# Transformer trunk on one core: first loads of the down matmul by units, the last gate unit's values in another buffer, and VectorE in place of GpSimd for four products' splits

## The chip, the core and the metric

The kernel runs on one NeuronCore of a Trainium2 chip. Five engines run side by side, each through its own list of instructions in strict order: TensorE (PE in the profile; its weight loads are PEld), VectorE (DVE), ScalarE (ACT), GpSimd (POOL), and SyncE (SP), whose list here holds nearly all transfers between HBM and the on-chip memory SBUF. They wait for one another by semaphores. The metric is the device time of one execution in microseconds; the median of several runs is compared.

## What is computed

A two-layer trunk over 1024 tokens of width 1024. Layer 0 mixes tokens by latent attention, layer 1 by differential attention; each mixer is followed by a layer norm, a SwiGLU feed-forward block with 2816 hidden values, and another layer norm. The change lies in the feed-forward block, which runs once per layer:

```python
def _swiglu(x, w_gu, w_down):
    gate, up = jnp.split(x @ w_gu, 2, axis=-1)
    return (jax.nn.silu(gate) * up) @ w_down

h = _layernorm(ALPHA * h + mix, ln_mix_g[i], ln_mix_b[i])
h = _layernorm(ALPHA * h + _swiglu(h, ffn_w_gu[i], ffn_w_down[i]), ln_ffn_g[i], ln_ffn_b[i])
```

Inputs and output are float32.

## The kernel before

**Splitting.** Each float32 operand of a matmul is split in two parts of the type float32r: ScalarE casts the value (the high part), another engine subtracts the cast from the value (the low part), and three matmuls (high by high, high by low, low by high) replace one. `split` (line 472) does this, and `op_unit` (479) does it into a fresh buffer of 128 x 2 x 512. The list `tags` says from which ring the buffer comes, by turns: "wh" and "wl" are rings of three buffers each in the pool `wp`, which lives through the whole kernel; "o" is a ring of six in a pool of the down matmul.

**Gate and up.** `ffn` (491) works a matrix product with seven products of blocks in place of eight. Its 22 units n (line 510 on) each have the products "1", "6", "2", "7", "5", "4", "3", of 12 matmuls each, taken from `stream` in an order of their own, with the weights of each split four steps ahead (`prepare`, 541, into "wh" and "wl"). The last product, "3", reads b22; "5" reads t1, "7" t3, "4" t4, and "1" and "2" read x (its first and its second half). `tmp[n]` (615) holds the unit's running values: 8 KB in each partition, from a ring of two ("ra" of `pool_a`). When a unit is through, `activations` (620) forms the hidden values of its half: L622 the silu on ScalarE, L626 and L627 two products on VectorE. After each second unit GpSimd forms four sums (L631 to L634, tile `sh`), and hidden values and sums go to HBM (`h_dr`, lines 636 and 637) in the blocks s = 0 to 6 that the down matmul asks for.

**Down.** Seven products again, each of 11 units j, and each unit of 12 matmuls: four blocks of 128 tokens by three. `from_h` (730) loads the hidden values of block s in groups of four, four and three units into a ring of two raw tiles (`rh`) and splits them, VectorE subtracting. The weights come from `b11` (751), `t1`, `t2`, `t3`, `block` ("b21", "b22") and `t4`. `b11` loads the eleven tiles `tt[j]`, 512 KB each, and splits the first half of each; `t1` subtracts one half of `tt[j]` from the other on VectorE (L758) and splits the difference; `t2` works on with `tt` (L764), and `t3` splits what it leaves. GpSimd subtracts for all of these except the first `early` = 3 units of `b11`. The names that the profile has for the seven products, in their order, are dx, dy, dx, dw, dv, dw, dw; all weights of the first, third and fifth appear as op_w_b, those of the others as op_w_t (in layer 1 the last has wt). `whole` (795) runs a product; `added` (804) adds a result to the rows z on VectorE, and `finish` does the layer norm.

**Memory.** A pool that is opened when others have been closed lies over their tiles. The raw tiles `rh` lie over one half of x, `tt0` to `tt3` over the other, `tt4` to `tt7` over the two buffers of `tmp`, `tt8` to `tt10` over t4; z, the "o" ring and the rows g and b lie over t2, t1, b22 and t3. A pool marked `reuse_waits="tile"` has its instructions wait for the old tiles under their own tile.

**Order.** The Tile framework plans each engine's list ahead of time: at each step the engine takes, among the instructions that its plan holds to be ready, the one that stands first in the program or has a higher priority (`tc.high_priority`). `behind` (155) adds that one instruction stands behind another in its list, without a wait. `load_down` (723) uses it to keep the loads of the down matmul in program order, as soon as `in_order` has been filled (834), which is after the first product. The first three units' loads and splits have a high priority. The rows g and b of the layer norm are broadcast into SBUF by two transfers on GpSimd's queue (832, 833).

Of the kernel before, what the change touches and what calls it, by code (L numbers as in the profile page):

```python
# [9 lines left out]
F32 = mybir.dt.float32  # L10
F32R = mybir.dt.float32r
AF = mybir.ActivationFunctionType
ALU = mybir.AluOpType
# [3 lines left out]
P = 128  # L17
S = 1024
D = 1024
# [23 lines left out]
def trunk(  # L43
# [63 lines left out]
    def f32(t):  # L107
        return t.bitcast(F32)
# [363 lines left out]
    def split(dst, src, eng):  # L472
        hi, lo = dst
        A.copy(hi, src)  # L474
        eng.tensor_tensor(lo, src, f32(hi), ALU.subtract)  # L475
# [15 lines left out]
    def ffn(side, xo, xst, pending, layer, x_src, x_dst, lng, lnb, next_x, spare=()):  # L491
# [212 lines left out]
        for i in (1, 0):  # L704
# [5 lines left out]
        poolx = stx.enter_context(tc.tile_pool(name=f"fx{layer}", bufs=1, side=swap(side), reuse_waits="tile"))  # L710
# [10 lines left out]
        chain, in_order, banks_read = [], [], []  # L721

        def load_down(dst, src):

            i = nc.sync.dma_start(dst, src).ins
# [25 lines left out]
        def b11():  # L751
            for j in range(11):
                load_down(tt[j], w_dn[layer, j].rearrange("p (b c) -> p b c", b=2))
                yield unit(tt[j][:, 0], f"b11_{j}", V if j < early else G)

        def t1():
            for j in range(11):
                V.tensor_tensor(tt[j][:, 0], tt[j][:, 1], tt[j][:, 0], ALU.subtract)  # L758
                yield unit(tt[j][:, 0], f"t1_{j}")
# [11 lines left out]
        def block(kh, cs, name):  # L771
            for j, r in enumerate(w_block(kh, cs, name)):
                yield unit(r, f"{name}_{j}")

        def t4():
            for j, r in enumerate(w_block(1, lo_half, "t4")):
# [6 lines left out]
                t = poolx.tile([P, 2, 512], F32R, tag=f"tt{j}", name=f"wt4{layer}_{j}")  # L783
# [69 lines left out]

        y4 = accumulators("w", "y")
# [638 lines left out]
```

## Time and profile before

| | us |
|---|---|
| median of 3 runs | 2299.32 |
| lowest and highest | 2297.55, 2300.04 |
| the profiled execution | 2302.24 |
| its span, first to last instruction | 2300.2 |
| mean granted TensorE clock | 0.993 |

The profile is of one execution. A timeline row has start, length, engine, line, operation, tiles written and read, shape and count, and in brackets the idle time of the engine before it with what ended that. Rows that follow each other are merged (x132), and a merged row lasts from the first start to the last end. Rows "SPq" are the issue of a transfer on SyncE's queue, not its duration. A group of instructions shows busy time and mean duration, or smallest, median and largest. Matmuls overlap: one is shown with 389 ns, and the next starts 227 ns after it where nothing holds it up, so pace is read from start to start.

The four engines' lists meet at the seam between the last gate unit and the first product of the down matmul, at about 873 us in layer 0 and 2071 us in layer 1.

### The profile page before, as it was taken

What the parts mean: (1) busy time and instruction counts of PE and PEld (TensorE: products, weight loads), DVE (VectorE), ACT (ScalarE), POOL (GpSimd) and SP (SyncE); (2) the same over time, 40 slices, a digit from 0 to 9 for tenths busy, and PEclk for the clock granted to TensorE, in tenths of its full rate; (3) what the DMA queues carried; (4) which work ended last, traced back from release to release, by engine and by line L of the source; (5) the groups of instructions that cost most, each with busy time, mean ns of one, the idle gap of its engine ahead of it and who ended that gap; (6) DMA issues with size and microseconds to landing.
All of it is one profiled execution on the core that took longest, in us unless ns stands there. A gap on an engine that the chain in (4) does not pass through costs nothing. (4 is left out here: it accounts for less than half of the span.)

```text
span 2300.2 us, 31168 instructions
## 1 busy us (share of the span) xinstructions
PE 2253.4 (98%) x11410; PEld 1919.6 (83%) x11410; DVE 1551.7 (67%) x2891; ACT 1017.8 (44%) x2096; POOL 863.9 (38%) x688
## 2 busy tenths in 40 slices
PE   8999999999999999999999999999999999999997
PEld 8899997878888887888888898987778888887886
DVE  5667664596666668667476667576586666658777
ACT  4455573342333324445365656555442333324453
POOL 2223241014444445555432424221014444435564
PEclk9999999999999999999999999999999999999999
DMA  5010125434435338544310212053344232337453
GB/s 200 14 36 30 41 72 180 138 128 142 178 133 197 128 111 327 198 171 156 94 54 19 70 38 69 16 214 139 108 160 149 76 120 87 125 127 284 160 205 121
DMA packets 105545, 288.28 MB, mean 125 GB/s; under 512 B 7968, under 2 KB 30112, under 8 KB 94896
## 3 DMA queue, kind: packets, MB, share of 16 engines
q1 hardware_dynamic: 100976, 275.87, 33.5%
q0 software_dynamic: 4416, 10.42, 1.7%
q8 instruction: 90, 1.47, 0.3%
q14 instruction: 63, 0.52, 0.1%
HBM read 205.00 MB, written 77.07 MB: 123 GB/s over the span
## 5 line engine op out<-in xcount | busy, mean ns | idle before, releaser
L474 ACT CAST op_g<-gr 128x512 fp32r<-128x512 f32 x240 | 147.0, 621 | 376.5 <-PE gb L520 188.4
L475 POOL TENSOR_TENSOR op_g<-gr,op_g 128x512 fp32r<-128x512 f32 x104 | 144.0, 1390 | 254.2 <-ACT op_g L474 140.7
L475 DVE TENSOR_TENSOR op_h<-rh,op_h 128x512 fp32r<-128x512 f32 x154 | 157.8, 1055 | 68.2 <-ACT op_h L474 68.2
L520 PE MATMUL ga<-xh_m,op_g 128*128 128x512 f32 x512 | 168.1, 389 | 0.0
L474 ACT CAST op_h<-rh 128x512 fp32r<-128x512 f32 x154 | 92.7, 619 | 147.5 <-PE dx L790 41.1
L790 PE MATMUL dw<-op_w_t,op_h 128*128 128x512 f32 x660 | 151.1, 390 | 0.0
L790 PEld LDWEIGHTS dw<-op_w_t,op_h 128*128 128x128 f32 x660 | 123.6, 188 | 25.6
L222 ACT ACTIVATE l_b<-l_b,mx_b 128x256 f32<-128x256 f32 (+7 forms) x128 | 99.5, 778 | 78.9 <-DVE mx_b L219 77.1
L1297 POOL TENSOR_SCALAR l_b<-l_b,r_b,cst 128x128 f32<-128x128 f32 (+3 forms) x64 | 52.8, 824 | 204.1 <-DVE r_b L224 193.5
L790 PE MATMUL dx<-op_w_b,op_h 128*128 128x512 f32 x528 | 124.4, 397 | 5.0 <-ACT op_w_b L474 3.9
L475 POOL TENSOR_TENSOR op_w_t<-tt,op_w_t 128x512 fp32r<-128x512 f32 x66 | 98.6, 1497 | 80.5 <-ACT op_w_t L474 79.9
L790 PEld LDWEIGHTS dx<-op_w_b,op_h 128*128 128x128 f32 x528 | 101.1, 192 | 28.0 <-ACT op_w_b L474 4.7
L475 DVE TENSOR_TENSOR op_g<-gr,op_g 128x512 fp32r<-128x512 f32 x136 | 111.4, 821 | 17.6 <-ACT op_g L474 17.4
L520 PE MATMUL gc<-b22h_f,op_g 128*128 128x512 f32 x352 | 115.6, 389 | 2.5 <-ACT op_g L474 2.5
L520 PE MATMUL gb<-t3h_f,op_g 128*128 128x512 f32 x352 | 115.6, 390 | 2.2 <-ACT tmp L622 1.6
L520 PE MATMUL gb<-t4h_f,op_g 128*128 128x512 f32 x352 | 115.8, 390 | 1.3 <-DVE tmp L603 1.3
L475 POOL TENSOR_TENSOR op_g<-s,op_g 128x512 fp32r<-128x512 f32 x40 | 54.6, 1365 | 166.0 <-ACT op_g L474 158.0
L520 PE MATMUL gc<-t1h_f,op_g 128*128 128x512 f32 x352 | 115.9, 390 | 0.6 <-ACT op_g L474 0.5
L520 PE MATMUL gb<-t2h_f,op_g 128*128 128x512 f32 x352 | 115.2, 390 | 0.4 <-DVE op_g L475 0.4
L520 PEld LDWEIGHTS ga<-xh_m,op_g 128*128 128x128 f32 x512 | 96.1, 188 | 20.0
L143 PE MATMUL bp<-xT_f,h_wb 128*128 128x512 f32 x256 | 103.7, 405 | 0.0
L145 PE MATMUL bp<-xT_f,l_wb 128*128 128x512 f32 x256 | 102.0, 399 | 0.0
(376 smaller groups left out, 6749.6 us busy)
## 6 DMA issues: line engine op xcount, KB each, us to landing
gr<-in_w_gu SPq DMA_DIRECT2D x44, 1024.0 KB, 6.9
rh<-h_dr SPq DMA_DIRECT2D x28, 1024.0 KB, 5.1
h_dr<-sh SPq DMA_DIRECT2D x22, 1024.0 KB, 5.0
h_dr<-hp SPq DMA_DIRECT2D x22, 768.0 KB, 4.1
tt<-in_w_dn SPq DMA_DIRECT2D x22, 512.0 KB, 7.9
rh<-h_dr SPq DMA_DIRECT2D x14, 768.0 KB, 4.3
wo_dr<-op_pwo SPq DMA_DIRECT2D x16, 512.0 KB, 3.4
z<-xs_dr SPq DMA_DIRECT2D x16, 512.0 KB, 10.1
```

Of the source, the lines that this page charges most:

```text
L143: T.matmul(ps_out, lh, rh, start=(i == 0), stop=False)
L145: T.matmul(ps_out, ll, rh, start=False, stop=(i == n - 1))
L222: A.activation(l[:, :n], l[:, :n], AF.Exp, bias=mx, scale=-1.0, accum_out=sm)
L474: A.copy(hi, src)
L475: eng.tensor_tensor(lo, src, f32(hi), ALU.subtract)
L520: T.matmul(o, w[:, a, kc], x[b][:, k, :], start=(first and k == 0 and (a, b) == (0, 0)), stop=(k == 3 and a == 1), skip_group_check=True,)
L790: T.matmul(o, h[:, a, c], w[:, b_], start=(first and (a, b_) == (0, 0)), stop=(last and a == 1), skip_group_check=True,)
L1297: G.tensor_scalar(l1[:, :n], l1[:, :n], r1, nlam, ALU.mult, ALU.mult)
```

## The change

- `from_h` can load unit by unit (`one`), 256 KB each in place of 1 MB, and the first product does so; its first `early` = 2 units, and those of `b11`, are split into the ring ("wh", "wl") alone. They are traced by turns, one of the hidden values and one of the weights, at a high priority.
- `tmp` of the last unit (n = 21) comes from the ring of five big tiles (`big_tile`, 8 KB each, which also holds the gate weights `gr`, `hp`, `sh` and later the raw weights `rw`).
- The eleven `tt` tiles come from two pools, one of eight and one of three, at the same places as before.
- `load_down` keeps program order from the first load on.
- VectorE subtracts for all splits of b11, t1, b21 and b22 (and `b11` also subtracts one half of `tt[j]` from the other, which `t1` did). GpSimd keeps t2, t3 and t4.
- The broadcasts of g and b are traced behind the third product, inside `tc.issue_after(turns["last"])`, which puts what is traced in the block on the engine of the given instruction behind that instruction; `turns["last"]` is the subtraction of the latest `op_unit`.

```diff
     def split(dst, src, eng):
         hi, lo = dst
         A.copy(hi, src)
-        eng.tensor_tensor(lo, src, f32(hi), ALU.subtract)
+        return eng.tensor_tensor(lo, src, f32(hi), ALU.subtract).ins
...
-        split((t[:, 0], t[:, 1]), src, eng)
+        i = split((t[:, 0], t[:, 1]), src, eng)
+        turns["last"] = i
         return t
...
         def new_tmp(n):
-            tmp[n] = pool_a.tile([P, 4, 512], F32, tag="ra", name=f"tmp{layer}_{n}", bufs=2)
+            if n == NFF - 1:
+                tmp[n] = big_tile(f"tmp{layer}_{n}", F32).rearrange("p a (b c) -> p (a b) c", b=2)
+            else:
+                tmp[n] = pool_a.tile([P, 4, 512], F32, tag="ra", name=f"tmp{layer}_{n}", bufs=2)
...
-        poolx = stx.enter_context(tc.tile_pool(name=f"fx{layer}", bufs=1, side=swap(side), reuse_waits="tile"))
+        poolx = [
+            stx.enter_context(tc.tile_pool(name=f"f{n}{layer}", bufs=1, side=swap(side), reuse_waits="tile"))
+            for n in "ex"
+        ]
+        js = [range(8), range(8, 11)]
+        if swap(side) != "left":
+            js = [reversed(r) for r in js]
...
         tt = {
-            j: poolx.tile([P, 2, 512], F32, tag=f"tt{j}", name=f"tt{layer}_{j}")
-            for j in (range(11) if swap(side) == "left" else reversed(range(11)))
+            j: p.tile([P, 2, 512], F32, tag=f"tt{j}", name=f"tt{layer}_{j}") for p, r in zip(poolx, js) for j in r
         }
...
             i = nc.sync.dma_start(dst, src).ins
-            if in_order:
+            if chain:
                 behind(i, chain[-1])
             chain.append(i)
...
-        def from_h(s, name, tags=tags):
+        def from_h(s, name, tags=tags, one=False):
             for gi, (j0, j1) in enumerate(groups):
                 r = poolh.tile([P, 4, 512], F32, tag="rawh", name=f"rh{layer}_{name}_{gi}")
-                load_down(r[:, :j1 - j0], h_dr[gi][s, :, :j1 - j0, :])
+                if not one:
+                    load_down(r[:, :j1 - j0], h_dr[gi][s, :, :j1 - j0, :])
                 for j in range(j0, j1):
-                    yield op_unit(r[:, j - j0], V, f"h{layer}_{name}_{j}", tags, pool)
+                    if one:
+                        load_down(r[:, j - j0], h_dr[gi][s, :, j - j0, :])
+                    yield op_unit(r[:, j - j0], V, f"h{layer}_{name}_{j}", ring if one and j < early else tags, pool)
...
         def b11():
             for j in range(11):
                 load_down(tt[j], w_dn[layer, j].rearrange("p (b c) -> p b c", b=2))
-                yield unit(tt[j][:, 0], f"b11_{j}", V if j < early else G)
+                w = unit(tt[j][:, 0], f"b11_{j}", V, ring if j < early else tags)
+                V.tensor_tensor(tt[j][:, 0], tt[j][:, 1], tt[j][:, 0], ALU.subtract)
+                yield w
 
         def t1():
             for j in range(11):
-                V.tensor_tensor(tt[j][:, 0], tt[j][:, 1], tt[j][:, 0], ALU.subtract)
-                yield unit(tt[j][:, 0], f"t1_{j}")
+                yield unit(tt[j][:, 0], f"t1_{j}", V)
...
         def block(kh, cs, name):
             for j, r in enumerate(w_block(kh, cs, name)):
-                yield unit(r, f"{name}_{j}")
+                yield unit(r, f"{name}_{j}", V)
...
-        early = 3
+        early, ring = 2, ("wh", "wl")
...
-        hs, ws = from_h(0, "1"), b11()
+        hs, ws = from_h(0, "1", one=True), b11()
         with tc.high_priority(100):
-            hs, ws = (itertools.chain([next(x) for _ in range(early)], x) for x in (hs, ws))
+            first = [(next(hs), next(ws)) for _ in range(early)]
+        hs, ws = (itertools.chain([u[i] for u in first], x) for i, x in enumerate((hs, ws)))
...
-        g = bcast_row(pool, lng, D, f"fg{layer}", "g")
-        b = bcast_row(pool, lnb, D, f"fb{layer}", "b")
-        in_order.append(True)
...
+        with tc.issue_after(turns["last"]):
+            g = bcast_row(pool, lng, D, f"fg{layer}", "g")
+            b = bcast_row(pool, lnb, D, f"fb{layer}", "b")
         y4 = accumulators("w", "y")
         whole(y4, from_h(4, "6"), t2(), True)
```

More of the change, by code (lines that the diff above doesn't have):

```diff
@@ L716, in ffn @@
         tt = {
-            j: poolx.tile([P, 2, 512], F32, tag=f"tt{j}", name=f"tt{layer}_{j}")
-            for j in (range(11) if swap(side) == "left" else reversed(range(11)))
+            j: p.tile([P, 2, 512], F32, tag=f"tt{j}", name=f"tt{layer}_{j}") for p, r in zip(poolx, js) for j in r
         }
-        chain, in_order, banks_read = [], [], []
+        chain, banks_read = [], []
         def load_down(dst, src):
             i = nc.sync.dma_start(dst, src).ins
-            if in_order:
+            if chain:
                 behind(i, chain[-1])
             chain.append(i)
-        def from_h(s, name, tags=tags):
+        def from_h(s, name, tags=tags, one=False):
             for gi, (j0, j1) in enumerate(groups):
                 r = poolh.tile([P, 4, 512], F32, tag="rawh", name=f"rh{layer}_{name}_{gi}")
-                load_down(r[:, :j1 - j0], h_dr[gi][s, :, :j1 - j0, :])
+                if not one:
+                    load_down(r[:, :j1 - j0], h_dr[gi][s, :, :j1 - j0, :])
                 for j in range(j0, j1):
-                    yield op_unit(r[:, j - j0], V, f"h{layer}_{name}_{j}", tags, pool)
+                    if one:
+                        load_down(r[:, j - j0], h_dr[gi][s, :, j - j0, :])
+                    yield op_unit(r[:, j - j0], V, f"h{layer}_{name}_{j}", ring if one and j < early else tags, pool)
         def w_block(kh, cs, name):
@@ L782, in t4 @@
                     continue
-                t = poolx.tile([P, 2, 512], F32R, tag=f"tt{j}", name=f"wt4{layer}_{j}")
+                t = poolx[j > 7].tile([P, 2, 512], F32R, tag=f"tt{j}", name=f"wt4{layer}_{j}")
                 split((t[:, 0], t[:, 1]), r, G)
```

## The prediction

> **What bounds the kernel now.** I read the page first, for the engine that sets the time, then the list of who waited for whom on TensorE, then TensorE's timeline at the places that the list names, and last the queues that feed those places.
>
> ```profile
> PE 2253.4 (98%) x11410; PEld 1919.6 (83%) x11410; DVE 1551.7 (67%) x2891; ACT 1017.8 (44%) x2096; POOL 863.9 (38%) x688
> ```
>
> ```profile
> PE dx L790 <- ACT op_w_b L474: 3.9, 2, 2.0
> ...
> PE dw L790 <- DVE z L806: 2.5, 2, 1.5
> ...
> PE dx L790 <- DVE op_h L475: 1.0, 1, 1.0
> ```
>
> TensorE is the bound: 2253.4 of 2300.2 us. Work that other engines save is worth nothing unless a wait of TensorE goes with it. Three of its waits stand in the down matmul, the only place that the diff touches. Its timeline there, the end of the gate and up products and then each product of the down matmul, layer 0 and then layer 1 (start, length, engine, line, tiles, count, idle time before):
>
> ```profile
> 872.99 0.39 PE L520 MATMUL gc<-b22h_f,op_g 128*128 128x512 f32 x1
> 875.33 32.24 PE L790 MATMUL dx<-op_w_b,op_h 128*128 128x512 f32 x132 [1.95 <-ACT op_w_b L474]
> 907.40 30.08 PE L790 MATMUL dy<-op_w_t,op_h 128*128 128x512 f32 x132
> 937.32 30.08 PE L790 MATMUL dx<-op_w_b,op_h 128*128 128x512 f32 x132
> ```
>
> ```profile
> 2070.98 0.39 PE L520 MATMUL gc<-b22h_f,op_g 128*128 128x512 f32 x1
> 2073.32 25.48 PE L790 MATMUL dx<-op_w_b,op_h 128*128 128x512 f32 x104 [1.95 <-ACT op_w_b L474]
> 2099.75 6.64 PE L790 MATMUL dx<-op_w_b,op_h 128*128 128x512 f32 x28 [0.95 <-DVE op_h L475]
> 2106.23 30.08 PE L790 MATMUL dy<-op_w_t,op_h 128*128 128x512 f32 x132
> ...
> 2257.49 1.63 PE L790 MATMUL dw<-wt,op_h 128*128 128x512 f32 x6 [1.49 <-DVE z L806]
> 2260.09 28.85 PE L790 MATMUL dw<-wt,op_h 128*128 128x512 f32 x126 [0.97 <-DVE z L806]
> ```
>
> A product without a wait takes 937.32 - 907.40 = 29.92 us from start to start, 0.227 for each of its 132 matmuls and 2.72 for each of its 11 units. From the second product on nothing is lost until the last. The first product alone is long: 907.40 - 875.33 = 32.07 us in layer 0 (2.15 too many), 2106.23 - 2073.32 = 32.91 in layer 1 (2.99 too many). Ahead of it 2.34 us pass from the last gate matmul's start to its own, where 0.23 would do: 2.11 lost in each layer. In all 2.11 + 2.15 + 2.11 + 2.99 = 9.36 us, 0.41% of the span; that is all the diff can win at this place.
>
> Part of what the first product loses is not waiting. Layer 1 once more, in stretches (PE busy with its matmuls, PEld, DVE, ACT and POOL busy, granted clock, DMA share, GB/s):
>
> ```profile
> 2073.30:2077.30 4.00, 3.98 (x11) 3.12 (x12) 3.96 (x4) 1.53 (x3) 3.58 (x3) 0.59 0.78 224
> 2077.30:2081.30 4.00, 4.00 (x19) 3.31 (x18) 3.97 (x5) 1.86 (x3) 2.67 (x2) 0.99 0.96 383
> ```
>
> For 4 us behind the 1.95 us of idling the clock was granted at 0.59, and 11 matmuls started where some 18 would. Of the 26.43 us up to 2099.75, 104 matmuls need 23.58 and the wait in front of the next, in the ninth unit, 1.11, so slow matmuls cost 1.74; the ninth unit's wait and its first matmuls take the other 2.99 - 1.74 = 1.25. The waits of 0.95 and 1.49 us show no such tail: six matmuls in 1.63 us is the full pace. So the first wait costs twice, its length and its tail.
>
> [...]
>
> **What the first product waits for.** ScalarE's and SyncE's rows in layer 1, then one of SyncE's and two of ScalarE's in layer 0:
>
> ```profile
> 2072.13 0.63 ACT L622 ACTIVATE tmp<-tmp 128x512 f32<-128x512 f32 x1 [2.25 <-DVE tmp L611]
> 2072.66 1.12 ACT L474 CAST op_w_b<-tt 128x512 fp32r<-128x512 f32 x2
> ```
>
> ```profile
> 2059.59 1.28 SPq L725 DMA_DIRECT2D tt<-in_w_dn  x3
> 2073.51 0.38 SPq L636 DMA_DIRECT2D h_dr<-hp  x1
> 2073.93 3.12 SPq L725 DMA_DIRECT2D tt<-in_w_dn  x5
> ```
>
> ```profile
> 862.53 0.80 SPq L725 DMA_DIRECT2D rh<-h_dr  x2
> ```
>
> ```profile
> 867.42 1.67 ACT L474 CAST op_h<-rh 128x512 fp32r<-128x512 f32 x3 [4.29 <-DMA rh<-h_dr]
> ...
> 875.47 0.62 ACT L474 CAST op_w_b<-tt 128x512 fp32r<-128x512 f32 x1 [0.20 <-DMA tt<-in_w_dn]
> ```
>
> In layer 1 the first three weight tiles were asked for 13 us before the first cast of one (2059.59, 2072.66), so it is not their landing. The cast stands behind L622 in ScalarE's strict order, and L622 behind the last gate unit. By the code its target is an "o" buffer, which lies over t2, t1, b22 and t3 and is planned as free only when the last gate product has read them. All eleven tt tiles are one pool, also over the last unit's values (tmp 21) and over t4, and in the planned order the rest of them stand behind the write of hp. In layer 0 the second tile really lands late, at 875.47, behind 2 MB of rh and 1 MB of broadcast rows.
>
> **The change, part by part.**
>
> *First two units in the ring "wh"/"wl", loads unit by unit.* The four splits no longer touch an "o" buffer. Their buffers were read last by the products 6, 2, 7 and 5 of the last gate unit; in both layers all four are over two products, 5.4 us, before the end. Their loads are 2 x (256 + 512) KB in place of 2 MB ahead of the first tt. In layer 0 the first MB had landed 4.9 us after its issue at 862.5 (cast at 867.42); at 383 GB/s 1.5 MB need 1.3 us more, so about 869, and with the broadcasts between some 870. A cast of 0.62 and a subtraction of 0.68 end by 871.5, before the last gate matmul is through at 873.2. Wait removed, with its tail: -2.11 -1.74 in layer 1. In layer 0 the first product lost 2.15 in all; the same tail, and 0.4 at its ninth unit: -2.11 -2.15. If the cover fails, one unit late by x costs x, and the tail from between 1.49 and 1.95 us on.
>
> *tmp 21 in a big tile, tt0 to tt7 in a pool of their own.* Without tmp 21 that pool lies over x and tmp 20 and 19 alone, free at the end of product 2, so eight pairs can be queued some 10 us before the end. 8 x 768 KB at 383 GB/s is 2.05 us a pair against 2.72 that TensorE takes: DMA keeps ahead, and the third group of rh, whose late arrival made the ninth unit wait, finds a shorter queue: -1.25 in layer 1 and the 0.4 above. The big pool has five buffers; tmp 21 takes the raw weights' of unit 20, whose last split is made before its product, and sh 10 moves one on, to hp 9's, written out long before. Nothing.
>
> *Order of loads from the first.* Everything in the chain stays in trace order on SP. Behind a load that waits (rh's unit 8 for a raw buffer, unit 10 for the write of hp) stand tt8 to tt10, the next rh and eight z loads. The first needs of those are unit 8 at +21.8 us and z at the product's end, +29.9; the writes end some 8 us in, and 9 MB at 383 GB/s take 24. Nothing, with about 5 us to spare at z.
>
> *issue_after for g and b.* It binds instructions on the engine of the last split, now VectorE; the two broadcasts are GpSimd's. I take it that they stay where they were; 1 MB, 2.7 us of DMA, is in the 870 above.
>
> *VectorE alone splits b11, t1, b21, b22.* 8 + 11 + 11 + 11 = 41 subtractions a layer leave GpSimd. What one costs VectorE depends on GpSimd:
>
> ```profile
> 2074.12 1.66 DVE L758 TENSOR_TENSOR tt<-tt 128x512 f32<-128x512 f32 x1
> 2075.70 1.76 DVE L475 TENSOR_TENSOR op_w_b<-tt,op_w_b 128x512 fp32r<-128x512 f32 x1
> 2077.39 1.78 DVE L475 TENSOR_TENSOR op_h<-rh,op_h 128x512 fp32r<-128x512 f32 x1
> 2079.09 0.68 DVE L758 TENSOR_TENSOR tt<-tt 128x512 f32<-128x512 f32 x1
> 2079.69 0.68 DVE L475 TENSOR_TENSOR op_w_b<-tt,op_w_b 128x512 fp32r<-128x512 f32 x1
> 2080.40 1.67 DVE L758 TENSOR_TENSOR tt<-tt 128x512 f32<-128x512 f32 x1
> ```
>
> ```profile
> 2073.57 1.66 POOL L631 TENSOR_TENSOR sh<-hp 128x512 f32<-128x512 f32 x1 [7.56 <-DVE hp L627]
> ...
> 2076.99 1.62 POOL L634 TENSOR_TENSOR sh<-hp,sh 128x512 f32<-128x512 f32 x1
> 2079.95 8.37 POOL L475 TENSOR_TENSOR op_w_b<-tt,op_w_b 128x512 fp32r<-128x512 f32 x5 [1.33 <-ACT op_w_b L474]
> ```
>
> ```profile
> 2196.00:2225.90 29.90, 29.90 (x133) 24.77 (x132) 21.47 (x21) 15.07 (x27) 22.40 (x15) 1.00 0.45 167
> 2225.90:2255.90 30.00, 30.00 (x133) 24.59 (x131) 29.17 (x42) 18.26 (x38) 16.97 (x13) 1.00 0.58 210
> ```
>
> ```profile
> L806 DVE SCALAR_TENSOR_TENSOR z<-z,dx x32: 672/674/689, 907.7 to 2174.5; 128x512 f32<-128x512 f32 x32
> ```
>
> While GpSimd works on a tile a subtraction takes 1.7 us, in its pauses 0.68 (0.60 from start to start). A unit of b11 asks VectorE for three: 2.0 us in quiet against 2.72. t1, b21 and b22 ask for two, 15 us a product, and 4 to 12 additions to z of 0.67, at most 8: 23 of 29.9. Covered by six pairs of buffers. The narrow place is the first 7.4 us, where GpSimd makes the last unit's sums and VectorE gets through three subtractions in 5 us. With TensorE's end as 0: L627 is through at 2.3; h of unit 2 fits in front of it; w of unit 2 is done by 4.0 (needed at 5.4), its tt by 5.7, w of unit 3 by 7.4 (needed at 8.2), unit 4 at 9.3 (needed at 10.9). Margins of 0.8 to 1.6. I charge 0.3 a layer, between 0 and 1.4 us of waiting with a tail of 1.74 (3.1).
>
> At the last product TensorE waits 1.49 and 0.97 us for VectorE's additions, in a stretch where VectorE is busy for 29.17 of 30.00. GpSimd's t3 splits may now come sooner and the queue be shorter: between -2.5 and +1; I take 0.
>
> **The sum:** -9.36 + 0.6 = -8.8 us on the profiled execution, whose span is 2300.2 and whose own time is 2302.2, 2.0 of it outside the span; the median of the runs is 2299.3, 2.9 below it. The same 8.8 from the median gives **2290.5**.
>
> **The rivals.**
> The 10 us before the first product in layer 1, in the same columns as above:
>
> ```profile
> 2061.00:2071.20 10.20, 9.55 (x42) 7.42 (x40) 4.90 (x8) 1.98 (x4) 1.16 (x2) 1.00 0.71 250
> ```
>
> 1. *The wait moves a few units on*, to VectorE's narrow place, in both layers. For it: margins below 1 us, and an order planned ahead that may put a tt subtraction first. Against it: VectorE is idle for half of that stretch, room for units 0 and 1 and more. Price 3.1 a layer: 2299.3 - 9.36 + 6.2 = 2296.1.
> 2. *The first wait stays*: the casts still stand behind L622. For it: ScalarE's order is strict. Against it: neither buffer nor data holds them there any longer. What is won is 1.25 + 0.4 alone: 2297.7.
> 3. *VectorE becomes the bound in the fifth product* (b22). It asks for 22 subtractions, 13.2 us in quiet, and four additions, 2.7; each that meets GpSimd's t3 splits costs 1.1 more. Beyond about 12 that meet, it passes 29.9; if all 22 do, 41.6, 11.7 late in each layer: 2299.3 - 9.36 + 23.4 = 2313.3. For it: the stretch at 2196 has 15 of GpSimd's. Against it: ten of those were b22's own, and go.
>
> [...]
>
> **How the numbers follow.** The forecast gets 0.68 (its own range 2287 to 2294), rival 1 0.14, rival 2 0.07, rival 3 and other ways to lose 0.11. About 0.2%, 4.6 us, is what this measurement can tell from none. Faster is the forecast and the better part of rival 1, 0.73; the same is the rest of rival 1 and rival 2, 0.15; slower 0.12. The range runs from 2285.5 (the sum without the charge and with 2.5 at the last product, and 2 for the spread of the runs) to 2298.5, past rivals 1 and 2.
>
> **What would show it.** Right: the first dx matmul follows the last gc at 0.23 us in both layers, the granted clock stays at 1.0 there, both first products take 29.9 to 31, the first four casts stand ahead of L622, eight tt loads ahead of the write of hp, and quiet 0.68 us subtractions in b11. Wrong: idle time of TensorE before dx behind op_h or op_w_b of units 2 to 4, a clock of 0.6 there, or any product of the middle longer than 29.9.

## The result and the profile after

The changed kernel takes 2305.22 us (median of 7 runs, 2301.50 to 2314.82) beside 2299.32 of the kernel before on the same chip (7 runs, 2296.57 to 2302.13). It is slower: by 5.9 us between the medians, and by a ratio of 1.0038, 95% interval 1.0028 to 1.0048, which is 6.4 to 11.0 us. The forecast was 2290.5, faster.

| | before | after |
|---|---|---|
| the profiled execution, us | 2302.24 | 2306.54 |
| its span | 2300.2 | 2304.8 |
| mean granted clock | 0.993 | 0.993 |

The busy times of the engines, from the page of the changed kernel, answer to the first line shown of before:

```profile
PE 2253.1 (98%) x11410; PEld 1919.9 (83%) x11410; DVE 1546.3 (67%) x2973; ACT 1017.5 (44%) x2096; POOL 749.1 (33%) x606
```

VectorE does 82 instructions more in 5.4 us less, and GpSimd is free of 115 us: in quiet the subtractions are quick, as was forecast (medians of 0.68 to 0.69 us for those of b11, t1, b21 and b22). TensorE's timeline says where the time goes. First layer 0, from the last matmul of the t3 product on (start, length, engine, line, tiles, count, idle time before; L521 is the gate matmul here, L804 that of the down matmul):

```profile
864.95 0.39 PE L521 MATMUL gb<-t3h_f,op_g 128*128 128x512 f32 x1
868.65 0.60 PE L521 MATMUL gb<-t4h_f,op_g 128*128 128x512 f32 x1 [3.31 <-DVE tmp L604]
...
873.09 1.07 PE L804 MATMUL dx<-op_w_b,op_h 128*128 128x512 f32 x4
...
876.49 0.39 PE L521 MATMUL gc<-b22h_f,op_g 128*128 128x512 f32 x1
876.72 29.18 PE L804 MATMUL dx<-op_w_b,op_h 128*128 128x512 f32 x128
905.73 11.04 PE L804 MATMUL dy<-op_w_t,op_h 128*128 128x512 f32 x48
918.00 19.34 PE L804 MATMUL dy<-op_w_t,op_h 128*128 128x512 f32 x84 [1.23 <-ACT op_h L474]
937.18 3.11 PE L804 MATMUL dx<-op_w_b,op_h 128*128 128x512 f32 x13
```

The wait in front of dx is gone: 0.23 us from the last gc to the dx behind it. But TensorE now waits *inside* the last gate unit. The t4 product starts 3.47 us late, its twelve matmuls take 4.44 us in place of 2.72 (1.72 lost to a slow clock, granted at 0.57 from 868.60 to 872.60), and the second product takes 31.45 in place of 29.92 (1.53). Layer 1 in the same columns:

```profile
2064.53 2.88 PE L804 MATMUL dx<-op_w_b,op_h 128*128 128x512 f32 x12
...
2073.60 1.98 PE L804 MATMUL dx<-op_w_b,op_h 128*128 128x512 f32 x8
2077.70 22.08 PE L804 MATMUL dx<-op_w_b,op_h 128*128 128x512 f32 x96 [2.12 <-ACT op_w_b L474]
2104.24 4.60 PE L804 MATMUL dx<-op_w_b,op_h 128*128 128x512 f32 x12 [4.46 <-ACT op_w_b L474]
2108.67 11.04 PE L804 MATMUL dy<-op_w_t,op_h 128*128 128x512 f32 x48
2120.94 19.33 PE L804 MATMUL dy<-op_w_t,op_h 128*128 128x512 f32 x84 [1.23 <-ACT op_h L474]
2140.11 2.20 PE L804 MATMUL dx<-op_w_b,op_h 128*128 128x512 f32 x9
```

Unit 0 of dx even runs between the gate products. Then come 2.29 us lost ahead of unit 2 (8 matmuls need 1.81 of the 4.10), 4.78 in the 96 matmuls up to unit 10 (26.54 us for 21.76), 1.71 in the slow ones behind (12 in 4.43, the clock granted at 0.57), 1.52 in the second product. The sum over both layers is 6.7 + 10.3 = 17.0 us, where before lost 9.36 at these places and 0.65 more in a t4 wait of layer 1 that the prediction did not count:

```profile
2065.65 0.47 PE L520 MATMUL gb<-t4h_f,op_g 128*128 128x512 f32 x1 [0.65 <-DVE tmp L603]
```

That is 7 us. The spans differ by 4.6 only. The rest is not of the change: up to the last gate unit of layer 0 the instructions stand in the same order in both kernels, and yet the two executions differ there by 2.6 us (the last matmul of the unit before it starts at 859.39 in the kernel before and at 856.79 in the changed one).

**Behind the 3.31 us.** ScalarE's and VectorE's rows in layer 0; L475 is the subtraction of a split, L604 the addition of product 7 that t4 waits for:

```profile
866.65 0.62 ACT L474 CAST op_h<-rh 128x512 fp32r<-128x512 f32 x1 [3.40 <-DMA rh<-h_dr]
```

```profile
867.30 0.69 DVE L475 TENSOR_TENSOR op_h<-rh,op_h 128x512 fp32r<-128x512 f32 x1 [8.01 <-ACT op_h L474]
867.91 0.68 DVE L604 TENSOR_TENSOR tmp<-tmp,gb 128x512 f32<-128x512 f32 x1
```

The t3 product was through at 865.3 and VectorE had been idle for 8 us. But its list has the first subtraction of op_h ahead of the addition, and that one waits for a cast, and the cast for a load that lands at 866.6. In the kernel before, the addition (L603 there) stands first and waits for the t3 product alone:

```profile
865.26 0.69 DVE L603 TENSOR_TENSOR tmp<-tmp,gb 128x512 f32<-128x512 f32 x1 [3.36 <-PE gb L520]
868.08 0.69 DVE L475 TENSOR_TENSOR op_h<-rh,op_h 128x512 fp32r<-128x512 f32 x1 [2.13 <-ACT op_h L474]
```

**Behind the 2.12 us.** ScalarE in layer 1; the casts of the weights of unit 2 and 3 are the row x2:

```profile
2076.51 0.62 ACT L474 CAST op_h<-rh 128x512 fp32r<-128x512 f32 x1 [6.17 <-DMA rh<-h_dr]
2077.03 1.14 ACT L474 CAST op_w_b<-tt 128x512 fp32r<-128x512 f32 x2
...
2079.12 0.63 ACT L627 ACTIVATE tmp<-tmp 128x512 f32<-128x512 f32 x1
```

ScalarE idles for 6.17 us for the hidden values of unit 5, which its list has ahead of the weights of unit 2. The silu (L627) stands behind too, and with it the write of hp.

**Behind the 4.46 us.** GpSimd, VectorE and SyncE's queue in layer 1. L636 is the first of the last four sums, L642 the write of the sums, and L735 behind it the first of the two loads of unit 10:

```profile
2082.15 10.10 POOL L636 TENSOR_TENSOR sh<-hp 128x512 f32<-128x512 f32 x1 [16.45 <-DVE hp L632]
```

```profile
2081.99 0.68 DVE L475 TENSOR_TENSOR op_w_b<-tt,op_w_b 128x512 fp32r<-128x512 f32 x1
2082.59 0.68 DVE L475 TENSOR_TENSOR op_h<-rh,op_h 128x512 fp32r<-128x512 f32 x1
...
2089.81 1.28 DVE L768 TENSOR_TENSOR tt<-tt 128x512 f32<-128x512 f32 x2
```

```profile
2082.09 0.37 SPq L641 DMA_DIRECT2D h_dr<-hp  x1
2095.01 0.37 SPq L642 DMA_DIRECT2D h_dr<-sh  x1
2095.48 1.30 SPq L735 DMA_DIRECT2D rh<-h_dr  x1
```

A sum that takes 1.3 to 1.7 us elsewhere takes 10.10: from 2081.99 to 2091.09 VectorE's subtractions follow each other every 0.60 us without a pause, and the sum ends 1.2 us behind the last of them. The write of the sums waits for it, and the loads of unit 10 stand behind that write on SP, though they need the write of hp alone.

All four losses have one form: an instruction that can go stands in its engine's list behind one that can't. The theory from here on is called "order"; its rivals are "transfers" (the loads are too late, whatever the lists) and "VectorE" (41 more subtractions a layer are too much for it).

### The profile page after: what moved, and what is told of

Its sections match the earlier page's. It is cut to its first block, busy times and chain, and to the rows that moved or that the text cites. A ratio compares the mean times of both kernels' runs of the same rounds, so it can differ in the third digit from the quotient of the medians.

```text
span 2304.8 us, 31101 instructions
## 1 busy us (share of the span) xinstructions
PE 2253.1 (98%) x11410; PEld 1919.9 (83%) x11410; DVE 1546.3 (67%) x2973; ACT 1017.5 (44%) x2096; POOL 749.1 (33%) x606
## 3 DMA queue, kind: packets, MB, share of 16 engines
q8 instruction: 90, 1.47, 0.3%
## 5 line engine op out<-in xcount | busy, mean ns | idle before, releaser
L475 POOL TENSOR_TENSOR op_g<-gr,op_g 128x512 fp32r<-128x512 f32 x104 | 144.3, 1392 | 251.7 <-ACT op_g L474 134.8
L475 DVE TENSOR_TENSOR op_h<-rh,op_h 128x512 fp32r<-128x512 f32 x154 | 123.9, 822 | 76.6 <-ACT op_h L474 76.6
L521 PE MATMUL ga<-xh_m,op_g 128*128 128x512 f32 x512 | 168.2, 389 | 0.0
L804 PE MATMUL dw<-op_w_t,op_h 128*128 128x512 f32 x660 | 151.2, 390 | 0.0
L804 PEld LDWEIGHTS dw<-op_w_t,op_h 128*128 128x128 f32 x660 | 123.7, 188 | 25.6
L475 POOL TENSOR_TENSOR op_w_t<-tt,op_w_t 128x512 fp32r<-128x512 f32 x44 | 65.6, 1492 | 239.7 <-ACT op_w_t L474 239.7
L804 PE MATMUL dx<-op_w_b,op_h 128*128 128x512 f32 x528 | 123.0, 393 | 6.6 <-ACT op_w_b L474 6.6
L804 PEld LDWEIGHTS dx<-op_w_b,op_h 128*128 128x128 f32 x528 | 100.1, 190 | 28.4 <-ACT op_w_b L474 7.4
L475 DVE TENSOR_TENSOR op_g<-gr,op_g 128x512 fp32r<-128x512 f32 x136 | 111.4, 821 | 17.6 <-ACT op_g L474 17.1
L521 PE MATMUL gb<-t4h_f,op_g 128*128 128x512 f32 x352 | 116.9, 393 | 4.1 <-DVE tmp L604 4.1
L521 PE MATMUL gc<-b22h_f,op_g 128*128 128x512 f32 x352 | 115.6, 389 | 1.9 <-ACT op_g L474 1.9
L521 PE MATMUL gc<-t1h_f,op_g 128*128 128x512 f32 x352 | 115.9, 390 | 0.6 <-ACT op_g L474 0.5
L521 PE MATMUL gb<-t2h_f,op_g 128*128 128x512 f32 x352 | 115.2, 390 | 0.4 <-DVE op_g L475 0.4
L521 PE MATMUL gb<-t3h_f,op_g 128*128 128x512 f32 x352 | 115.2, 389 | 0.0
L521 PEld LDWEIGHTS ga<-xh_m,op_g 128*128 128x128 f32 x512 | 96.1, 188 | 19.9
L475 POOL TENSOR_TENSOR op_g<-s,op_g 128x512 fp32r<-128x512 f32 x40 | 54.7, 1367 | 165.9 <-ACT op_g L474 157.9
## 6 DMA issues: line engine op xcount, KB each, us to landing
z<-xs_dr SPq DMA_DIRECT2D x16, 512.0 KB, 10.3
```

The lines of the kernel that those rows point to most:

```text
L475: return eng.tensor_tensor(lo, src, f32(hi), ALU.subtract).ins
L521: T.matmul(o, w[:, a, kc], x[b][:, k, :], start=(first and k == 0 and (a, b) == (0, 0)), stop=(k == 3 and a == 1), skip_group_check=True,)
L804: T.matmul(o, h[:, a, c], w[:, b_], start=(first and (a, b_) == (0, 0)), stop=(last and a == 1), skip_group_check=True,)
```

## The experiments

All ran beside the kernel before, in three series, with these medians of 5 to 12 runs and these ratios to it:

| run | us | before | ratio, 95% interval |
|---|---|---|---|
| add_first | 2304.65 | 2298.09 | 1.0036, 1.0023 to 1.0049 |
| sums_write_last | 2301.59 | 2298.09 | 1.0015, 1.0006 to 1.0024 |
| gpsimd_back | 2308.47 | 2298.09 | 1.0043, 1.0030 to 1.0056 |
| seam_pinned | 2295.76 | 2298.09 | 0.9988, 0.9980 to 0.9997 |
| seam_and_casts | 2286.58 | 2298.66 | 0.9946, 0.9934 to 0.9958 |
| seam_and_casts_gpsimd | 2298.60 | 2298.66 | 1.0001, 0.9992 to 1.0009 |
| before_with_pools | 2303.60 | 2298.66 | 1.0021, 1.0012 to 1.0031 |
| after_without_pools | 2309.62 | 2298.66 | 1.0048, 1.0036 to 1.0060 |
| casts_in_order | 2309.24 | 2298.33 | 1.0044, 1.0031 to 1.0057 |
| sums_on_vectore | 2300.28 | 2298.33 | 1.0006, 0.9997 to 1.0016 |
| seam_groups | 2290.25 | 2298.33 | 0.9966, 0.9953 to 0.9979 |
| seam_no_pools | 2297.30 | 2298.33 | 1.0001, 0.9990 to 1.0012 |

The changed kernel ran in a series of its own, with 1.0038, 1.0028 to 1.0048. By these intervals add_first, gpsimd_back, after_without_pools and casts_in_order can't be told from it in time; what they show is read from their profiles.

### One wait at a time

**add_first.**

```diff
-                V.tensor_tensor(u3, p1, acc[n, "b"], ALU.add)
+                turns["add7"] = V.tensor_tensor(u3, p1, acc[n, "b"], ALU.add).ins
...
+                    if one and j == 0:
+                        behind(turns["last"], turns["add7"])
...
```

> The changed kernel with one thing more: in VectorE's list the first subtraction for the hidden values (op_h, unit 0) stands behind the addition of product 7 of the last gate unit. Theory 'order': in layer 0 this subtraction waits for a transfer that lands at 866.6 and holds up that addition, and with it TensorE for 3.31 us ahead of the t4 product and 1.7 us of slow matmuls behind. Without it the t4 product follows the t3 product at once; the first four dx matmuls, planned ahead of the last gate product, then wait 0.5 to 1.0 us for their weights. Expected 4 to 4.5 us less than the changed kernel (2305.2): 2300.7 to 2301.2; layer 1 as it was. Rival 'transfers': the first loads are what is late, so the wait only moves to the four dx matmuls, 2.5 us or more there, and under 1.5 us is won.

The wait went as expected, 3.31 to 0.78 us and no slow matmul (the twelve of t4 in 2.86), and the gain did not come: 2304.65. TensorE in layer 0:

```profile
864.35 0.39 PE L521 MATMUL gb<-t3h_f,op_g 128*128 128x512 f32 x1
865.51 0.50 PE L521 MATMUL gb<-t4h_f,op_g 128*128 128x512 f32 x1 [0.78 <-DVE tmp L604]
...
901.04 3.03 PE L807 MATMUL dx<-op_w_b,op_h 128*128 128x512 f32 x12 [1.42 <-ACT op_w_b L474]
904.17 11.24 PE L807 MATMUL dy<-op_w_t,op_h 128*128 128x512 f32 x48
```

From the last t3 matmul to the second product are 39.82 us, where the changed kernel has 40.78. TensorE came to unit 10 earlier, and unit 10's loads went out later, at 892.47 in place of 890.50, since a sum of 8.30 us now stood ahead of them in layer 0 as well. The next late thing ate most of the gain: in layer 0 TensorE now loses 1.75 us on the way to unit 10 and 0.41 behind it, where the changed kernel loses nothing. Two short waits for the weights of unit 2, 0.25 and 0.29 us, came up too. The rival's figure (under 1.5 us won) came true, but not for its reason: the four dx matmuls had their weights.

**casts_in_order.** In `split`, while the first product is traced:

```diff
-        A.copy(hi, src)
+        i = A.copy(hi, src).ins
+        if turns.get("casts") is not None:
+            if turns["casts"]:
+                behind(i, turns["casts"][-1])
+            turns["casts"].append(i)
```

> The changed kernel with one thing more: ScalarE's casts of the first product stand in the order of the units. Theory 'order': the wait of 2.12 us at unit 2 of layer 1 (the cast of unit 5 stands ahead of it) goes, but the last unit's loads still stand behind the write of the sums, so most of it comes back in the wait at unit 10; the silu moves up 1 to 2 us. Layer 0's 3.31 us stays. 2302 to 2305.5 beside 2305.2. Rival 'VectorE': the wait at unit 2 stays, since VectorE is what is late there.

In layer 1 the wait at unit 2 went and that at unit 10 stayed (4.39 us), as expected. The time, 2309.24, lies above the expected range. In layer 0 GpSimd's first sum, which took 1.67 us in the changed kernel, now took 11.89. GpSimd's row there, and VectorE's at the end of the run:

```profile
879.94 11.89 POOL L640 TENSOR_TENSOR sh<-hp 128x512 f32<-128x512 f32 x1 [14.64 <-DVE hp L636]
```

```profile
890.01 0.69 DVE L479 TENSOR_TENSOR op_w_b<-tt,op_w_b 128x512 fp32r<-128x512 f32 x1
890.73 1.66 DVE L772 TENSOR_TENSOR tt<-tt 128x512 f32<-128x512 f32 x1
```

VectorE pauses for a few hundredths of a us at 890.7, the subtraction behind the pause takes 1.66, and the sum ends 1.1 us behind it, at 891.83. A new wait of 2.22 us at unit 10 of layer 0, with slow matmuls (12 in 4.44), costs 4.1 us there, more than the 2.3 that layer 1 won.

**sums_write_last.**

```diff
-                nc.sync.dma_start(d[:, 3:7], t)
+                turns["sh"] = nc.sync.dma_start(d[:, 3:7], t).ins
...
         whole(x4, hs, ws, True)
+        behind(turns["sh"], chain[-1])
```

> The changed kernel, with the write of the last sums (sh) placed behind the last load of b11 in SyncE's list. Theory 'order': in layer 1 GpSimd's first sum takes 10.1 us, the write of the sums waits for it until 2095.0, and the last unit's two loads stand behind that write; TensorE waits 4.46 us at unit 10 and runs slow for 1.6 us more. With the write out of the way the loads wait for the write of hp alone, go out some 4 us sooner, and the wait and its tail go: 5 to 6 us less, 2299.2 to 2300.2, while the sum still takes about 10 us. Layer 0 as it was. Rival 'VectorE': the unit is late because VectorE is behind with its splits, and the wait stays above 2 us.

```profile
2087.27 0.32 SPq L735 DMA_DIRECT2D rh<-h_dr  x1
2095.81 0.37 SPq L642 DMA_DIRECT2D h_dr<-sh  x1
```

SyncE's queue in layer 1: unit 10 is loaded 8.2 us sooner. TensorE in layer 1:

```profile
2077.82 24.79 PE L804 MATMUL dx<-op_w_b,op_h 128*128 128x512 f32 x108 [2.23 <-ACT op_w_b L474]
2104.05 11.22 PE L804 MATMUL dy<-op_w_t,op_h 128*128 128x512 f32 x48 [1.44 <-ACT op_h L474]
2137.91 4.47 PE L804 MATMUL dx<-op_w_b,op_h 128*128 128x512 f32 x19
```

108 matmuls run to the second product without a wait, though the sum still took 10.10 us. The second product then begins 1.44 late and takes 33.86 in place of 31.44, so 3.9 of the 6.5 came back in this profile, which is of the slowest of the 11 runs. Why the second product lost more was not followed up. 2301.59 is a little above the expected range, and "VectorE", which held that the wait at unit 10 would stay, is wrong.

**sums_on_vectore.** In `activations`, and so for all four sums:

```diff
-                G.tensor_tensor(t[:, 0], h21, h22, ALU.add)
+                E = V if j == 10 else G
+                E.tensor_tensor(t[:, 0], h21, h22, ALU.add)
```

> The changed kernel with the four sums of the last hidden pair on VectorE in place of GpSimd, 8 x 0.6 us more for it in all. Theory 'order': no sum waits for GpSimd's turn, the last unit's two loads stand ahead of the write of the sums in layer 1, and its wait of 4.46 us with 1.6 of slow matmuls goes or falls below 1 us although VectorE has more to do; layer 0's 3.31 stays. 2298 to 2302. Rival 'VectorE has too much to do': the wait stays or grows, 2305 or more.

The same from the other side: the wait and its tail at unit 10 of layer 1 are gone with more work on VectorE; 2300.28, as expected. That speaks against "VectorE".

### Parts of the change undone, or done alone

**gpsimd_back.** In t1 and in `block` likewise:

```diff
-                w = unit(tt[j][:, 0], f"b11_{j}", V, ring if j < early else tags)
+                w = unit(tt[j][:, 0], f"b11_{j}", V if j < early else G, ring if j < early else tags)
```

> The changed kernel with GpSimd subtracting again for t1, b21, b22 and for b11 from the third unit on, as before. Theory 'order': the 3.31 and 1.7 us of layer 0 and the 2.1 us at unit 2 of layer 1 stay, as the lists are the same there; the last sums are spread between GpSimd's splits and their write stands behind five loads more in layer 1, so the wait at unit 10 (4.46 and 1.6) goes or falls below 2 us; VectorE gets more of its subtractions at 1.7 us. Expected 2299 to 2303. Rival 'VectorE is overloaded by the 41 subtractions': the kernel falls below the one of before, 2295 or less.

2308.47 fits neither. In layer 1 the wait at unit 2 is gone, against expectation; unit 10 waits 2.72 us for VectorE in place of 4.46, and the fourth product has a new wait of 2.06. Both are waits for op_h. At unit 10 VectorE is late: beside GpSimd's splits its subtractions take 1.78 us each, one behind the other, from 2078.76 on. Work given back to GpSimd makes VectorE late there, where the changed kernel's VectorE was not. At the fourth product VectorE is idle, for a load, and op_h stands behind:

```profile
2183.61 5.89 DVE L778 TENSOR_TENSOR tt<-rw_t,tt 128x512 f32<-128x512 f32 x6 [2.50 <-DMA rw_t<-in_w_dn]
```

That is a side effect of the edit. `turns["last"]` is now a subtraction of GpSimd's, so `issue_after` binds the broadcasts of g and b, 1 MB, behind it: in layer 1 they go out at 2154.43 in place of 2064.54, 1 us ahead of the second load of t2's raw weights (rw_t). This load then takes 11.4 us in place of 7.2, and the third, for which VectorE waits, goes out 9.2 us behind the product's start in place of 4.9. So this wait need not come of who splits.

**before_with_pools** and **after_without_pools.** The lines of the change for tmp 21, the two pools and t4 put in, and taken out; of the latter:

```diff
-                tmp[n] = big_tile(f"tmp{layer}_{n}", F32).rearrange("p a (b c) -> p (a b) c", b=2)
+            tmp[n] = pool_a.tile([P, 4, 512], F32, tag="ra", name=f"tmp{layer}_{n}", bufs=2)
```

> The kernel before, with tmp 21 in a big tile and the eleven tt tiles in two pools, and nothing else of the change. Theory 'order': the weight casts come ahead of the silu and all eleven tt loads ahead of the write of hp, and no early split stands ahead of a gate addition, so the wait of 1.95 us and its tail shrink; what is left is unit 0's subtraction behind the last gate addition (0.5 to 1.5 us) and the third group of hidden values behind both writes. 2294 to 2299 beside 2298.1. Rival: this part of the change is the one that loses, over 2301.

> The changed kernel with tmp 21 and the eleven tt tiles where they were before. Theory 'order': the weight casts stand behind the silu again, so the wait of some 2 us in front of the first product and its tail come back, and the loads from unit 2 on stand behind the write of hp, those from unit 4 on behind the write of the sums. Slower than the changed kernel: 2305 to 2312. Rival, the big tile and the pools are what lost: at or below the kernel before.

Alone, this part costs 5 us: the rival came true. Its profile has 0.78 us ahead of t4, 0.71 and 0.89 in the first unit and 1.55 at unit 8 of layer 0, behind the 1 MB loads and both writes. Taken from the changed kernel it gives 2309.62, in the expected range, with the old 1.95 us back in front of dx in both layers; that it costs 4.4 us there is not shown, since the intervals overlap. What a part does hangs on the lists that it gives.

### The order written out

**seam_pinned.** To the edits of casts_in_order and sums_write_last come these (`turns` keeps the instructions meant: "mm" the last gate matmul, "add5" the addition of product 5, "hp" L632):

```diff
+                if turns.get("mm") is not None:
+                    behind(i, turns["mm"])
...
+                    if one and j == 0:
+                        behind(turns["last"], turns["add5"])
+                    if one and j == early:
+                        behind(turns["last"], turns["hp"])
+                        behind(turns["casts"][-1], turns["silu"])
```

> The changed kernel with the order at the seam written out: the dx matmuls behind the last gate matmul; the first subtraction of op_h behind the addition of product 5; casts of the first product in the order of the units, those from unit 2 on behind the last silu and their subtractions behind the last product hp; the write of the last sums behind the last load of b11. VectorE still splits for all four products, and no buffer, transfer size or engine differs from the changed kernel. Theory 'order': the three waits and their slow matmuls (3.3 + 1.7 in layer 0, 2.1 + 4.5 + 1.6 in layer 1) go, 13 us in all less 0 to 3 for what comes up in their place: 2292 to 2295, below the kernel before. Rival 'transfers': weights of units 0 to 2 land too late, waits come back ahead of them, and over 2300 is left. Rival 'VectorE': waits for op_h or op_w_b of units 3 to 9, and 2297 to 2301.

2295.76: 9.5 us below the changed kernel, by the medians of two series, a little under the kernel before (0.3 to 2.0 per mille), just above the expected range. The first products take 30.9 and 29.92 us, dx follows gc at 0.23, and all sums of the last hidden values take 1.7. The second product still takes 31.45.

**seam_and_casts.** From `from_h` (the same in `b11`), from `product` (`after` is the last matmul of product 7 where n is 21 and this is product 5) and from the place up to which casts are kept in order:

```diff
-                    if one and j == 0:
+                    if one and j < early:
                         behind(turns["last"], turns["add5"])
...
+                    if after is not None:
+                        behind(turns["mm"], after)
...
         whole(x4, from_h(6, "3"), block(1, hi_half, "b22"), True)
+        turns["casts"] = None
```

> seam_pinned with four orders more: all subtractions of units 0 and 1 behind the addition of product 5; product 5 of the last gate unit behind its product 7; the casts of the next four products also in the order of their units. Theory 'order': what is left in seam_pinned is again a matter of lists: t4 for the addition just ahead of it (0.78 us in each layer), one wait of 0.67 at unit 3 of layer 0, the second product in both layers (1.23 and its slow restart, 1.5 longer than 29.92, behind five weight casts that each wait for a free buffer), the fourth and fifth in layer 0 (1.06 and 0.65 longer than 29.92). Together 7 us: 2287 to 2292 (seam_pinned 2295.8), and all products of the middle take 29.9. Rival 'VectorE': these waits come from too much work, and turn up elsewhere; 2294 to 2297.

2286.58, the best of all: 12.1 us below the kernel before and, by the medians of two series, 18.6 below the changed one, without another buffer, engine or transfer than that has. TensorE, layer 0 and layer 1:

```profile
870.96 0.39 PE L525 MATMUL gc<-b22h_f,op_g 128*128 128x512 f32 x1
871.19 30.23 PE L819 MATMUL dx<-op_w_b,op_h 128*128 128x512 f32 x132
901.25 30.08 PE L819 MATMUL dy<-op_w_t,op_h 128*128 128x512 f32 x132
```

```profile
2061.29 30.08 PE L819 MATMUL dx<-op_w_b,op_h 128*128 128x512 f32 x132
2091.21 30.08 PE L819 MATMUL dy<-op_w_t,op_h 128*128 128x512 f32 x132
```

dx follows gc at 0.23, the seam costs nothing any more, and the first products take 30.06 and 29.92. Why the second product's 1.5 us were an order too shows on ScalarE in the changed kernel, layer 0, where the hidden values of unit 4 stand behind five weight casts, the last four of which wait 2.1 us each for TensorE to give a buffer back, and have no wait of their own:

```profile
908.65 0.62 ACT L474 CAST op_w_t<-tt 128x512 fp32r<-128x512 f32 x1 [2.10 <-PE dy L804]
...
916.81 0.62 ACT L474 CAST op_w_t<-tt 128x512 fp32r<-128x512 f32 x1 [2.09 <-PE dy L804]
917.33 3.22 ACT L474 CAST op_h<-rh 128x512 fp32r<-128x512 f32 x6
```

From that kernel each part of the change was then taken away, with the edit of gpsimd_back, with `from_h(0, "1")` in place of `from_h(0, "1", one=True)`, and with that of after_without_pools; the orders stay written out:

> seam_and_casts with GpSimd subtracting again for t1, b21, b22 and for b11 from the third unit on. Theory 'order': with the lists written out the engine of the splits is worth little; the last sums stand between GpSimd's splits and are done later, and VectorE runs at 1.7 us more often. 1 to 6 us slower than seam_and_casts. Rival 'the 41 subtractions on VectorE are themselves a loss': faster than seam_and_casts by 2 or more.

> seam_and_casts with the hidden values of the first product loaded in groups of four, four and three units again, 1 MB for the first. Theory 'order': with the lists written out the size of the first loads is worth little: the first four weight tiles and the first group need 3 MB before unit 3, there by then, and no wait comes back ahead of units 0 to 3. Within 2 us of seam_and_casts: 2285 to 2289. Rival 'transfers': the unit-by-unit loads are what the gain rests on; waits ahead of units 0 to 4, over 2290.

> seam_and_casts with tmp 21 and the eleven tt tiles where they were before. Theory 'order': the first weight cast stands behind the silu again and the loads from unit 2 on behind the write of hp, so the wait of some 2 us in front of the first product comes back in both layers, with or without its slow matmuls: 4 to 9 us slower than seam_and_casts, 2290 to 2296. Rival, the place of tmp 21 is worth nothing (as the prediction had it): within 2 us of seam_and_casts.

GpSimd's splits back: 2298.60, 12 us lost, twice the most that was expected. Some 5.7 us of it lie in the down matmuls: waits of 0.38 for op_h at unit 10 in both layers, and 3.0 in the fourth product of layer 1, where the broadcasts stand in front of rw_t again (a load of 11.2 us and a wait of 2.03). Most of the rest lies between the layers, where the edit touches nothing: TensorE is busy for 958.96 us there, beside 953.17 in seam_and_casts, with as many matmuls but for one. So what the engine of the splits is worth by itself stays open.

Loads in groups: 2290.25, some 4 us lost, more than expected, but not at the first units, where the rival had it: dx follows gc at once and takes 30.1 and 29.92 us. A wait of 1.01 comes up in the second product of layer 0, and one of 2.53 in the last of layer 1; the latter need not be of the edit, as the same wait is 2.41 in sums_write_last and 3.08 in sums_on_vectore.

Tiles where they were: 2297.30, 11 us lost, a little more than expected, at the place that was expected. TensorE there, layer 0:

```profile
871.10 3.91 PE L811 MATMUL dx<-op_w_b,op_h 128*128 128x512 f32 x16 [1.95 <-ACT op_w_b L474]
876.99 2.11 PE L811 MATMUL dx<-op_w_b,op_h 128*128 128x512 f32 x8 [1.98 <-DVE op_w_b L479]
```

With the lists written out, each of the three parts is missed when it is taken away; for the tiles alone is the whole loss found at the seam.

## Why the prediction was wrong

**What can be won here, 9.36 us: right.** seam_and_casts loses 0.14 us in the two first products and 0.75 in the fourth and fifth of layer 0: 8.5 of the 9.36 are won, where the sum had 8.8. The t4 wait of layer 1 is gone too. The rest of its 12.1, which the runs know to 2.8 either way, lies outside the down matmul and was not followed up.

**"Wait removed": the step that failed.** The prediction worked out that the cast and the subtraction of the first unit end by 871.5, before TensorE wants them, and stopped there. It did not ask what stands *behind* that subtraction on VectorE while it waits for its load, as it did ask for SP. The addition of product 7 does, and t4 behind that: 5.2 us in layer 0.

**VectorE's narrow place, 0.3 us a layer: wrong engine.** The charge held GpSimd to be the one that slows VectorE. In layer 1 it was GpSimd's first sum that was slow, at 10.10 us beside VectorE's subtractions of 0.68, and no wait there was for a late VectorE. The wait at unit 2 that rival 1 had foreseen came (2.29 us), by ScalarE's list and not by VectorE. The price of rival 1, 3.1 a layer, was too low there, with 8.8 lost in the first product, since the sum of 10.10 us held up a write and two loads.

**"Order of loads: nothing".** It had "the writes" end some 8 us in. In layer 1 the write of the sums went out at 2095.01, 21.6 us behind the last gc, with unit 10's loads behind it: 4.78 and 1.71 us. The cover of 5 us was that of z; unit 10's own was not worked out.

**"Any product of the middle longer than 29.9"** was named as a sign of failure, and came in the second product, 1.53 and 1.52, by ScalarE's list (and with 0.38 in the fifth of layer 0, which was not followed up in the changed kernel).

**"tmp 21 in a big tile, tt0 to tt7 in a pool of their own"** got 1.65 us for the ninth unit's waits, and the first wait went to the ring "wh"/"wl" alone. But seam_no_pools has that ring and the loads unit by unit, and yet the silu ahead of the first weight cast and the 1.95 us: it is the tiles that bring the weight casts ahead of the silu (11 us beside seam_and_casts). Alone they lose 5.

**Rival 3's price** was added up wrongly: with its own 0.60 and 1.1 us for each of 22 subtractions and 2.7 for the additions it is 40.1 and not 41.6, and so 2310.3. Nothing hung on it.

**Right:** the first four casts stand ahead of the silu and eight pairs of loads ahead of the write of hp; quiet subtractions of 0.68; the two broadcasts stay where they were; no product is bound by VectorE (rival 3); the last product's waits stay (1.47 and 0.97 beside 1.49 and 0.97). Rival 2 fell.

## What to carry to other kernels

An instruction that is moved up and waits takes its whole engine with it (here VectorE for 8.01 us and ScalarE for 6.17): for each engine that it touches, list what now stands behind it, and who waits for that, before its own finish is worked out. When a planner orders the lists, a new buffer or priority changes orders that nobody wrote; if removing one wait wins nothing, look for the next late thing, and pin the few orders that matter all together. Only then can the parts of a change be judged one by one.

## What the runs showed of the hardware

GpSimd's first sum of 128 x 512 took 10.10 us in the rows above, with 15 of VectorE's subtractions back to back beside it; it took 8.30 in layer 0 of add_first, 10.10 in layer 1 of sums_write_last and 11.89 in casts_in_order. In seam_and_casts it took 1.67, and the VectorE subtraction beside it 1.79:

```profile
873.97 1.67 POOL L643 TENSOR_TENSOR sh<-hp 128x512 f32<-128x512 f32 x1 [9.55 <-DVE hp L639]
```

```profile
874.40 1.79 DVE L479 TENSOR_TENSOR op_w_b<-tt,op_w_b 128x512 fp32r<-128x512 f32 x1
```

That subtraction, started at 874.40, ends 0.55 us behind the sum's end at 875.64; in the changed kernel the subtractions beside the sum of 10.10 us took 0.68. Open is why the sum took 1.67 us at 873.97 here and at 880.80 in layer 0 of the changed kernel, where VectorE's rows show no pause either.

Slow matmuls behind a short wait come and go. The stretches behind the waits of 3.31, 2.12 and 4.46 us of the changed kernel (PE, PEld, DVE, ACT and POOL busy, granted clock, DMA share, GB/s):

```profile
868.60:872.60 4.00, 3.95 (x10) 3.16 (x11) 3.10 (x5) 1.24 (x2) 0.00 (x0) 0.57 1.03 400
2077.60:2081.60 4.00, 3.90 (x17) 3.23 (x18) 4.00 (x8) 4.00 (x9) 0.00 (x0) 1.00 1.04 416
2104.20:2108.20 4.00, 3.96 (x10) 3.16 (x11) 3.98 (x7) 4.00 (x8) 0.00 (x0) 0.57 1.01 414
```

The kernel before had the slow clock behind 1.95 us in both layers, 0.59 in layer 1 and 0.58 in layer 0:

```profile
875.30:879.30 4.00, 3.97 (x11) 3.12 (x12) 3.96 (x4) 1.76 (x3) 3.56 (x3) 0.58 0.95 300
```

In the changed kernel 2.12 us have none, nor have the 1.95 and 1.98 of seam_no_pools in layer 0 (16 matmuls in 3.91 us, 8 in 2.11). So the tail of 1.74, which the prediction's sum took as part of each such wait, depends on more than the length of the wait. The clock records of two profiles, of the kernel before and of the changed one, have these figures: up to the end of the work each slow stretch lasts 3.41 us, or twice that, at 0.50, and in each of the two profiles all of them begin whole multiples of 3.41 us apart. Counted in these steps, in the last gate unit and the down matmul, TensorE idled for 1.95 us in the step ahead of either slow stretch of the kernel before, and for 3.15 and 3.12 us in the changed kernel; the 2.12 fell 1.65 and 0.47 on two steps, and no slow one came behind either. No limit for a step's idle time follows from that: between those places of the two layers, in the changed kernel, one with 1.92 us, from 1561.82 on, had no slow one behind it, and one with 1.78, from 1514.03 on, had. What decides is not shown.
